# Seven products of a Strassen pair in another order, overlapped with the next pair

## The chip, the cores and the metric

The kernel runs on one core of a Trainium2 chip. The time is device microseconds (us) of one execution of the whole program, lower is better. The engines are named as in the profile: PE is TensorE (PEld its weight loads), DVE is VectorE, ACT is ScalarE, POOL is GpSimd, SP is SyncE, whose queue issues nearly all DMAs. Matmul results land in PSUM, which has eight banks of 128 x 512 floats per core in this kernel's use; all else lives in SBUF or in DRAM.

## The reference, cut to what matters

Two layers of a decoder trunk over 1024 tokens of width 1024, float32. Each layer normalises, projects with one wide matrix, runs four mLSTM heads and four retention heads of width 256, gates them and projects back:

```python
h = rmsnorm(x, norm_g[l]) * (1.0 + scale[:, None, :]) + shift[:, None, :]
p = h @ w_in[l]
mq, mk, mv, mo, mz, mi, mf, rq, rk, rv, rz = split_cols(p)
...
y_m = jax.nn.sigmoid(mo) * head_layernorm(cell, gn_m[l], N_HEADS_MLSTM) * jax.nn.silu(mz)
...
y_r = head_layernorm(ret, gn_r[l], N_HEADS_RET) * jax.nn.silu(rz)
y = jnp.concatenate([y_m, y_r], axis=-1) @ w_out[l]
x = x + gate[:, None, :] * y
```

`cell` and `ret` are chunkwise recurrences over q, k and v. mLSTM's q and k pass a causal convolution of four taps and SiLU first; retention's q and k are rotated by tables of sine and cosine.

## The kernel before, in words

**Precision.** Every float32 product is made of three matmuls on rounded operands (`mm3`): high x high, high x low, low x high. A weight tile is loaded into an `R` tile, `high` (ACT, L381) rounds it into a `wH` tile, `low` (DVE or POOL, L386) puts the rest into another `R` tile. There are 12 `R`, 5 `wH` and 12 `acc` tiles (`acc` is the pool for all 128 x 512 working tiles).

**A pair.** The projection `h @ w_in` is done by pairs of 128-wide column blocks against two halves of 512 tokens, with the contraction of 1024 cut in two. That is a 2 x 2 by 2 x 2 block product, and it is made with seven block products instead of eight (Strassen, in Winograd's form). A product is 4 k-tiles x 3 matmuls of 128 x 512. The weight sides are a11, a12, a22 and sums S1 to S4; the token sides are blocks of h and sums U1 to U4, made once per layer by `build_forms`. Two of the weight sums (S1, S3) are formed by DMAs that accumulate, issued on POOL (L661); S2 and S4 are formed in place by DVE (`total`, L665).

The seven products run into accumulating PSUM banks. `ORDER` says which: X takes a11, then S2, then S3, then a22; Y takes a12; Z takes S1, then S4. After some of them the bank's content so far is copied into an `acc` tile `keep` (ACT, L721) or added with a kept one (DVE, L724 for a12, L728 for S3, L731 for S4), and the sums go on to what uses them: `conv_chain` (ACT L832, DVE L838, L840), `rot_done` (L911 to L913), `z_gate` and `o_gate` (ACT L789 and L798, DVE L791 and L800). The next product into the same bank must wait until the copy or the sum has read it. In a pair X is written by products 1, 3, 5, 7 and Z by 4 and 6, so one product of another bank lies between two of the same. The sum of S3 goes to a fourth bank, those of a12 and S4 stay in theirs. All come from one pool of four banks (`pp`). For values (`vpair_units`) two pairs of heads go side by side, each product in two parts of 24 matmuls of 128 x 256, with three banks per part; `store` (L742 to L751) splits them and writes them to DRAM.

**The order of work.** `plan` lists the pairs (`v` values, `z` and `a` gates, `q` and `k`). `Feeder` turns it into events by product number: loads 7 or 8 products ahead, sums, rounding 3 ahead, low parts 2 ahead. After each product `tick` lets every pending generator do a step: `attention` (one row of `TABLE` per tick, four chunks a head), the chains, `gate_chain` (sums of the mLSTM gates, L503 to L561), `rotary_tables` (L427 to L452), `adaptive`. PE runs exactly in the order written; the instructions of the other engines are put in order by a scheduler that works on priorities (program order, with `tc.high_priority()` ahead) and its own estimate of time. Each engine then runs its queue in order.

**Retention's output.** `values` leaves a chunk's 128 x 256 result in a bank of the other pool (`pa`, four banks); `normalise` takes mean and variance from there (DVE L1119), gets the root from POOL, and ACT scales from the bank (L1139).

**The output projection.** `out_units` takes 16 pieces per half of the tokens and half of the columns (`cc`). `OutLoads.stage` makes a piece when it is taken: it loads the weight tile, rounds it, and with `cc == 0` loads y and its gate (L1208, L1209), multiplies them (DVE L1211), rounds (ACT L1214) and takes the rest (DVE L1215).

Of the kernel before, what the change touches and what calls it, by code (L numbers as in the profile page):

```python
# [11 lines left out]
F32 = mybir.dt.float32  # L12
# [3 lines left out]
ALU = mybir.AluOpType  # L16
# [71 lines left out]
def tile_hybrid_trunk(ctx, tc, x, xt, c, positions, w_ada, b_ada, norm_g, w_in, w_blk, w_val, conv_w, conv_b,  # L88
# [28 lines left out]

    def ps_p():
        return pp.tile([P, 512], F32, tag="p", name=nm("pp"))
# [356 lines left out]
    def gate_chain(l, pgs, gt):  # L476
# [20 lines left out]
        yield 1  # L497
# [125 lines left out]
    NAMES = ("a11", "a12", "S2", "S1", "S3", "S4", "a22")  # L623
    VNAMES = ("a12", "a11", "S2", "S1", "S3", "S4", "a22")
    POOL_LOW = ("S1", "S3", "a22")
    ORDER = (("X", "11"), ("Y", "21"), ("X", "U2"), ("Z", "U1"), ("X", "U3"), ("Z", "22"), ("X", "U4"))
    VORDER = (("Y", "21"), ("X", "11"), ("X", "U2"), ("Z", "U1"), ("X", "U3"), ("Z", "22"), ("X", "U4"))

    class Feeder:
        def __init__(self, now, jobs):  # L630
            self.events, self.forms, self.now = [], [], now
            t = 0
            for add in jobs:
                t = add(self, t)
            self.events.sort(key=lambda e: e[0])
            self.run()
# [9 lines left out]
        def take(self):  # L646
            return self.forms.pop(0)()

        def quad(self, names, blk, t0, u):
            raw, r, h = {}, {}, {}  # L650
            at = {n: t0 + u * i for i, n in enumerate(names)}
# [21 lines left out]
            T2, T4 = at["S2"], at["S3"]  # L673
            ev(T2 - 8, load, "S1", a21)
            ev(T2 - 6, add, "S1", a22)
            ev(T4 - 8, load, "S3", a21)
            ev(T4 - 6, add, "S3", a11)
            for n, src in (("a11", a11), ("a12", a12), ("a22", a22)):
                ev(at[n] - 7 + u, load, n, src)
            for n in names:  # L680
                if n not in ("S2", "S4"):
                    ev(at[n] - 4 + u, hi, n)
                    ev(at[n] - 2, lo, n, G if n in POOL_LOW else V)
            ev(T2 - 4, total, "S2", "a11", "S1")
            ev(T2 - 3, total, "S4", "a12", "S2")
            for n in ("S2", "S4"):
                ev(at[n] - 4 + u, hi, n)
                ev(at[n] - 2, lo, n, V)
            return r, h

    def pair_forms(l, cols2):
        def add(feed, t0):
            blk = [[w_block(l, c, kh) for kh in range(2)] for c in cols2]
            r, h = feed.quad(NAMES, blk, t0, 1)
            feed.forms += [lambda n=n: tiles4(h[n], r[n]) for n in NAMES]
            return t0 + len(NAMES)
        return add

    def vpair_forms(l, heads):
        def add(feed, t0):  # L700
            got = [feed.quad(VNAMES, [[w_val[l, h, kh * 2 + kp] for kh in range(2)] for h in heads], t0, 2)
# [943 lines left out]
```

## Time and profile before

| | |
|---|---|
| time, median of 3 runs (lowest to highest) | 2394.66 us (2390.65 to 2397.98) |
| the profiled execution | 2393.12 us, of which 2391.4 us are the span of the profile |
| PE busy | 2162.7 us, 90% |
| DVE busy | 1820.0 us, 76% |
| ACT busy | 1124.9 us, 47% |
| POOL busy | 948.8 us, 40% |
| granted TensorE clock, mean | 0.962 |
| DMA | 448.32 MB, mean 187 GB/s |

A row of a profile names the line, the engine, the operation and its tiles as out<-in, then busy time and the mean of one instruction; behind the bar stand the idle time of the engine before these instructions and what ended it. In a timeline the idle time before a group stands in square brackets. Lines that begin with SPq are DMA issues.

The span falls into a start (0 to 112 us), layer 0's pairs (to 1011), its output projection (to 1240), layer 1's first projections and gates (to 1300), its pairs (to 2174) and its output projection (to the end).

### The profile page before, as it was taken

To read this page: it belongs to the slowest core of one execution; us is meant where nothing else is said; L and a number is where in the kernel's file an instruction comes from. 1 tells how busy PE (TensorE), PEld (TensorE's weight loads), DVE (VectorE), ACT (ScalarE), POOL (GpSimd) and SP (SyncE) were. 2 spreads that over 40 slices of the span, in tenths; PEclk is the share of its full clock that TensorE was granted. 3 is DMA by queue.
4 is the path that set the end of the run, shared out by engine and by line. 5 is a ranking of instruction groups with operands and counts; after the bars stand their busy time and mean duration, and the time that the engine had idled before them with its cause. 6 is when DMAs were issued, how large, how long until landed. Compare 5 with 4: busy or idle time off the path is not lost. (4 is left out here: it accounts for less than half of the span.)

```text
span 2391.4 us, 35265 instructions
## 1 busy us (share of the span) xinstructions
PE 2162.7 (90%) x11483; PEld 1845.9 (77%) x11483; DVE 1820.0 (76%) x3301; ACT 1124.9 (47%) x2093; POOL 948.8 (40%) x842
## 2 busy tenths in 40 slices
PE   5869999898998999898898799999999999999978
PEld 4668889787897777776686788978977877787756
DVE  5898788979879888763538789788797788977263
ACT  6634334344554565542355334443555555654243
POOL 0333244444443444414165434544544344450303
PEclk8989999999999999999899899999999999999989
DMA  7247678777686667565532686876866666768582
GB/s 249 70 118 227 200 209 250 197 212 203 179 241 160 176 186 202 160 225 195 180 123 75 192 231 167 235 199 173 229 182 173 187 194 180 198 182 245 156 239 100
DMA packets 452549, 448.32 MB, mean 187 GB/s; under 512 B 191218, under 2 KB 309754, under 8 KB 452364
## 3 DMA queue, kind: packets, MB, share of 16 engines
q1 hardware_dynamic: 432636, 410.14, 55.7%
q0 software_dynamic: 19584, 35.66, 9.8%
q8 instruction: 90, 1.47, 0.3%
q14 instruction: 95, 0.78, 0.1%
q10 hardware_dynamic: 144, 0.26, 0.0%
HBM read 322.69 MB, written 123.24 MB: 186 GB/s over the span
## 5 line engine op out<-in xcount | busy, mean ns | idle before, releaser
L155 PE MATMUL pp<-b,wH 128*128 128x512 f32 x1616 | 649.5, 402 | 69.2 <-ACT acc L721 23.4
L156 PE MATMUL pp<-b,wH 128*128 128x512 f32 x1616 | 642.9, 398 | 13.0 <-DVE b L1215 13.0
L157 PE MATMUL pp<-b,R 128*128 128x512 f32 x1616 | 641.5, 397 | 0.0
L381 ACT CAST wH<-R 128x512 fp32r<-128x512 f32 x616 | 376.3, 617 | 451.5 <-PE pp L156 220.4
L386 POOL TENSOR_TENSOR R<-R,wH 128x512 fp32r<-128x512 f32 x276 | 386.8, 1407 | 459.5 <-ACT wH L381 350.3
L155 PEld LDWEIGHTS pp<-b,wH 128*128 128x128 f32 x1616 | 310.7, 192 | 149.5 <-ACT acc L721 38.1
L386 DVE TENSOR_TENSOR R<-R,wH 128x512 fp32r<-128x512 f32 x340 | 278.1, 820 | 159.0 <-ACT wH L381 124.8
L155 PE MATMUL pp<-wH,b 128*128 128x256 f32 (+1 forms) x1024 | 316.5, 309 | 57.3 <-ACT acc L771 19.2
L156 PEld LDWEIGHTS pp<-b,wH 128*128 128x128 f32 x1616 | 310.9, 192 | 73.6 <-DVE b L1215 15.0
L157 PEld LDWEIGHTS pp<-b,R 128*128 128x128 f32 x1616 | 310.2, 192 | 67.7
L156 PE MATMUL pp<-R,b 128*128 128x256 f32 (+1 forms) x1024 | 315.6, 308 | 22.4 <-DVE R L386 22.2
L157 PE MATMUL pp<-wH,b 128*128 128x256 f32 (+1 forms) x1024 | 314.1, 307 | 0.6 <-DVE b L1215 0.6
L155 PEld LDWEIGHTS pp<-wH,b 128*128 128x128 f32 x1024 | 205.3, 200 | 68.4 <-ACT acc L771 20.7
L156 PEld LDWEIGHTS pp<-R,b 128*128 128x128 f32 x1024 | 205.9, 201 | 31.6 <-DVE R L386 26.3
L157 PEld LDWEIGHTS pp<-wH,b 128*128 128x128 f32 x1024 | 205.6, 201 | 7.0 <-DVE b L1215 1.9
L826 POOL TENSOR_TENSOR kc<-acc,kc 128x512 fp32r<-128x512 f32 x64 | 91.0, 1422 | 200.4 <-ACT kc L825 183.5
L661 POOL DMA_DIRECT2D R<-in_w_blk_dram x104 | 92.3, 887 | 139.4 <-DMA R<-in_w_blk_dram 88.8
L838 DVE SCALAR_TENSOR_TENSOR acc<-pp,cols,acc 128x510 f32<-128x510 f32 (+2 forms) x192 | 139.0, 737 | 5.6 <-ACT acc L832 5.5
L826 POOL TENSOR_TENSOR q<-acc,q 128x512 fp32r<-128x512 f32 x64 | 92.6, 1447 | 81.7 <-ACT q L825 80.2
L1031 POOL TENSOR_TENSOR sL<-acc,sH 128x384 fp32r<-128x384 f32 (+1 forms) x64 | 70.8, 1106 | 107.2 <-ACT sH L1030 53.6
L665 DVE TENSOR_TENSOR R<-R,R 128x512 f32<-128x512 f32 x136 | 103.1, 758 | 3.7 <-DMA R<-in_w_blk_dram 1.9
L1054 ACT CAST cH<-cf 128x512 fp32r<-128x512 f32 (+1 forms) x80 | 49.7, 621 | 91.4 <-DVE cf L1051 67.9
(334 smaller groups left out, 4123.0 us busy)
## 6 DMA issues: line engine op xcount, KB each, us to landing
R<-in_w_blk_dram SPq DMA_DIRECT2D x276, 256.0 KB
vdr<-acc SPq DMA_DIRECT2D x128, 256.0 KB
ring<-vdr SPq DMA_DIRECT2D x64, 512.0 KB
R<-in_w_out_dram SPq DMA_DIRECT2D x128, 256.0 KB
R<-in_w_blk_dram POOLq DMA_DIRECT2D x104, 256.0 KB, 4.6
R<-in_w_val_dram SPq DMA_DIRECT2D x80, 256.0 KB
gdr<-acc SPq DMA_DIRECT2D x64, 256.0 KB
acc<-in_w_ada_dram SPq DMA_DIRECT2D x64, 256.0 KB
```

Source lines behind the costliest of these rows:

```text
L155: PE.matmul(o, lt[0], rt[0], start=start, stop=False, skip_group_check=more)
L156: PE.matmul(o, lt[0], rt[1], start=False, stop=False, skip_group_check=more)
L157: PE.matmul(o, lt[1], rt[0], start=False, stop=stop, skip_group_check=more)
L381: A.copy(h, r)
L386: eng.tensor_tensor(lo, r, f(h), ALU.subtract)
L661: G.dma_start(raw[n], src, accum_op=ALU.add)
L665: V.tensor_tensor(raw[n], raw[one], raw[two], ALU.add)
L826: eng.tensor_tensor(dst[1], src, f(dst[0]), ALU.subtract)
L838: V.scalar_tensor_tensor(acc[:, d:], pt[:, 0:HALF - d], wcol, acc[:, d:], ALU.mult, ALU.add)
L1031: G.tensor_tensor(lo, src, f(hi), ALU.subtract)
L1054: A.copy(new[0][:, :, 0:W], cf[:, :, 0:W])
```

## The change

- **Order of the products.** `slot_order` replaces `ORDER`: a11 (X), S1 (Z), the a22 of the pair before (its X), S2 (X), a12 (Y), S4 (Z), S3 (X), and then the next pair. So a pair's a22 comes two products into the next pair. Where values or nothing follow, the pair ends with S3, S4, a22 and has no overlap at its end. Two products of others now lie between two of the same X bank (one at the end of a pair that no pair follows), three between those of Z.
- **Banks.** The pool of four becomes two X banks and two for Y and Z. The sums of S3 and S4 go into the `keep` tiles in SBUF, not to a bank; the chains read them there.
- **Events.** `Feeder` and `quad` take the product numbers from `slot_order`; S4's weight sum is now made after a12 is loaded, from S2's tile.
- **Values.** a22 comes before S4; the a12 product's bank is given back after its sum.
- **Attention** of a head starts 4 instead of 6 ticks after its k pair's last product, which is a22.
- **Retention** copies the result out of the `pa` bank (ACT) into the `n` tile, and `normalise` works on that.
- **Gate sums and rotary tables** start later in the program's order: `gate_chain` pauses 7 ticks instead of 1, `rotary_tables` starts 7 ticks later.
- **Output pieces.** `OutLoads.stage` is split into `fetch` (the loads) and `make` (the arithmetic). Taking a piece keeps two made and three more fetched; the first two are fetched five products before the pairs end and one is made three before.

```diff
+    def ps_x():
+        return pp.tile([P, 512], F32, tag="x", bufs=2, name=nm("px"))
+
+    def ps_z():
+        return pp.tile([P, 512], F32, tag="z", bufs=2, name=nm("pz"))
...
-        yield 1
+        yield 7
...
-    ORDER = (("X", "11"), ("Y", "21"), ("X", "U2"), ("Z", "U1"), ("X", "U3"), ("Z", "22"), ("X", "U4"))
+    PRODUCT = {"a11": ("X", "11"), "S1": ("Z", "U1"), "S2": ("X", "U2"), "a12": ("Y", "21"), "S4": ("Z", "22"),
+               "S3": ("X", "U3"), "a22": ("X", "U4")}
+    VNAMES = ("a12", "a11", "S2", "S1", "S3", "a22", "S4")
+
+    def slot_order(kinds):
+        slots, held = [], []
+        for j, kind in enumerate(kinds):
+            if kind == "v":
+                slots += [(j, n, part) for n in VNAMES for part in range(2)]
+                continue
+            follow = j + 1 < len(kinds) and kinds[j + 1] != "v"
+            slots += [(j, "a11", 0), (j, "S1", 0)] + held + [(j, "S2", 0), (j, "a12", 0)]
+            slots += [(j, n, 0) for n in (("S4", "S3") if follow else ("S3", "S4", "a22"))]
+            held = [(j, "a22", 0)] if follow else []
+        return slots
...
             with tc.high_priority():
-                if n in (0, 2, 3):
+                if n in ("a11", "S1", "S2"):
                     keep[n] = wt("acc", 512, NACC)
-                    A.copy(keep[n], bank["Z" if n == 3 else "X"])
-                elif n == 1:
-                    c = keep[0] if loose else bank["Y"]
-                    V.tensor_tensor(c, bank["Y"], keep[0], ALU.add)
+                    A.copy(keep[n], bank[b])
+                elif n == "a12":
+                    c = keep["a11"] if loose else bank["Y"]
+                    V.tensor_tensor(c, bank["Y"], keep["a11"], ALU.add)
                     done(0, 0, c)
-                elif n == 4:
-                    c = ps_p()
-                    V.tensor_tensor(c, bank["X"], keep[3], ALU.add)
-                    done(1, 1, c)
-                elif n == 5:
-                    V.tensor_tensor(bank["Z"], bank["Z"], keep[2], ALU.add)
-                    done(0, 1, bank["Z"])
+                elif n == "S3":
+                    V.tensor_tensor(keep["S1"], bank["X"], keep["S1"], ALU.add)
+                    done(1, 1, keep["S1"])
+                elif n == "S4":
+                    V.tensor_tensor(keep["S2"], bank["Z"], keep["S2"], ALU.add)
+                    done(0, 1, keep["S2"])
...
-                    src[tt] = po[:, 0:HD]
+                    src[tt] = nrm[j][:, tt, :]
+                    A.copy(src[tt], po[:, 0:HD])
...
         def take(self):
-            self.stage()
+            self.make(2 - len(self.ready))
+            self.fetch(3 - len(self.fetched))
             return self.ready.pop(0)
...
-            launch(rotary_tables())
+            launch(rotary_tables(), 7)
...
+            if sum(left.values()) == 5:
+                loads.fetch(2)
+            elif sum(left.values()) == 3:
+                loads.make()
+            left[j] -= 1
+            if left[j] == 0 and jobs[j][0] == "k":
+                launch(attention(l, jobs[j][1][0], gt), 4, 1)
```

The built programs have the same number of instructions on every engine but ACT, which gets the 64 copies of the retention results. Of the DVE instructions, 204 of 128 columns by about 512 now read two SBUF tiles where they read a PSUM bank and an SBUF tile: 96 taps of the convolution, 28 gate products, 80 products and sums of the rotation and the value split. How the queues move is shown at three places. The line numbers of the changed kernel are higher (L381 becomes L390, L386 L395, L721 L743, L1139 L1158, L1208 L1226).

The first is ACT's queue around one retention q pair of layer 0. The copies (L721, L743) read X and Z; `wH` rows are roundings of weights, `n` rows the retention result, the others attention. Before:

```order
L721 COPY acc_5179<-pp_5166 128x512
L1054 CAST cH_5145<-cf_4719 128x2x256
L381 CAST wH_5300<-R_5160 128x512
L381 CAST wH_5339<-R_5221 128x512
L1139 ACTIVATE n_5134<-pa_5135,nmu_5242,rsd_5199 128x256
L721 COPY acc_5267<-pp_5166 128x512
L1030 CAST sH_5296<-acc_5203 128x384
L1054 CAST cH_5284<-cf_4719 128x2x256
L381 CAST wH_5362<-R_5253 128x512
L721 COPY acc_5320<-pp_5307 128x512
```

And in the changed kernel:

```order
L743 COPY acc_5121<-px_5108 128x512
L1122 COPY n_5139<-pa_5140 128x256
L1072 CAST cH_5151<-cf_4719 128x2x256
L390 CAST wH_5243<-R_5039 128x512
L743 COPY acc_5183<-pz_5170 128x512
L390 CAST wH_5304<-R_5168 128x512
L1158 ACTIVATE n_5139<-n_5139,nmu_5229,rsd_5194 128x256
L390 CAST wH_5345<-R_5106 128x512
L743 COPY acc_5259<-px_5108 128x512
L1048 CAST sH_5298<-acc_5198 128x384
L1122 COPY n_5139<-pa_5275 128x256
```

The copies come in the order a11, S1, S2 now, so that the two from X have Z's between them, and the retention result is taken from its bank by a copy of its own; the scaling that needs `nmu` from DVE still stands in the same queue, ahead of a bank copy.

The second is DVE's queue at layer 0's first value products, with the gate sums (tiles `q`, `kc`, `nd`, `cH`), the token sums (`acc` from `acc`), the weight sums and low parts (`R`) and the first sum of a bank. Before:

```order
L518 COPY cH_1320<-nd_1276 4x512
L520 SCALAR_TENSOR_TENSOR q_1223<-ones,nd_1276 4x512
L512 TENSOR_SCALAR q_1224<-kc_1225 4x512
L665 TENSOR_TENSOR R_1332<-R_1332,R_1340 128x512
L386 TENSOR_TENSOR R_1441<-R_1340,wH_1439 128x512
L613 TENSOR_TENSOR acc_1258<-acc_1258,acc_1256 128x512
L430 TENSOR_SCALAR acc_1196<-acc_1196,kc 128x256
L522 COPY cH_1320<-q_1223 4x512
L523 TENSOR_TENSOR nd_1276<-dm_1226,q_1223 4x512
L514 TENSOR_TENSOR kc_1225<-kc_1225,q_1224 4x512
```

And in the changed kernel:

```order
L527 COPY cH_1584<-nd_1483 4x512
L529 SCALAR_TENSOR_TENSOR q_1219<-ones,nd_1483 4x512
L521 TENSOR_SCALAR q_1220<-kc_1221 4x512
L686 TENSOR_TENSOR R_1303<-R_1303,R_1307 128x512
L395 TENSOR_TENSOR R_1397<-R_1307,wH_1395 128x512
L622 TENSOR_TENSOR acc_1254<-acc_1254,acc_1252 128x512
L792 TENSOR_TENSOR pz_1337<-pz_1337,acc_1424 128x512
L531 COPY cH_1584<-q_1219 4x512
L532 TENSOR_TENSOR nd_1483<-dm_1222,q_1219 4x512
L523 TENSOR_TENSOR kc_1221<-kc_1221,q_1220 4x512
```

The gate sums stand where they stood, between the same weight sums and low parts; the first step of the rotary tables (L430) is gone from here, and the sum of the first value bank (L792, before L772) has come up by 14 rows to this place.

The third is SP's queue in layer 0's output projection, where the pieces of the second half of the tokens begin: `R` rows are weight tiles, `ndr` and `gdr` rows y and its gate, `xdr` rows stores of the residual. Before:

```order
L376 DMA R_12366<-in_w_out_dram 128x512
L376 DMA R_12413<-in_w_out_dram 128x512
L376 DMA R_12440<-in_w_out_dram 128x512
L376 DMA R_12467<-in_w_out_dram 128x512
L1208 DMA acc_12419<-ndr_4_1_100 128x512
L1209 DMA acc_12420<-gdr_4_0_1_140 128x512
L1208 DMA acc_12446<-ndr_4_1_100 128x512
L1209 DMA acc_12447<-gdr_4_1_1_142 128x512
```

And in the changed kernel:

```order
L385 DMA R_12172<-in_w_out_dram 128x512
L1303 DMA xdr_89<-acc_12089 128x512
L385 DMA R_12190<-in_w_out_dram 128x512
L1303 DMA xdr_89<-acc_12098 128x512
L1226 DMA acc_12336<-ndr_4_1_100 128x512
L1227 DMA acc_12337<-gdr_4_0_1_140 128x512
L1303 DMA xdr_89<-acc_12107 128x512
L385 DMA R_12208<-in_w_out_dram 128x512
L1226 DMA acc_12358<-ndr_4_1_100 128x512
```

Before, the first y and gate of the half stood behind 15 weight loads of the column half that runs ahead of it; now 15 weight loads follow them before the fifth piece's y.

217 lines of the change are left out of this document (114 added, 103 removed).

## The prediction

> **What bounds the kernel now.** I read the page's busy times first, then the waits of PE, then the stages.
>
> ```profile
> span 2391.4 us, 35265 instructions
> PE 2162.7 (90%) x11483; PEld 1845.9 (77%) x11483; DVE 1820.0 (76%) x3301; ACT 1124.9 (47%) x2093; POOL 948.8 (40%) x842
> ```
>
> PE is busy nine tenths of the span, and the change gives it the same matmuls. What can be won is its idle time, 2391.4 - 2162.7 = 229 us, and matmuls run at a low clock. The stages (columns: length, busy us and instructions of PE, PEld, DVE, ACT, POOL, then the granted clock and the DMA share):
>
> ```profile
> 112.00:182.00 70.00, 44.98 (x313) 44.05 (x314) 68.24 (x113) 21.95 (x42) 27.14 (x19) 0.80 0.41 120
> 182.00:1011.00 829.00, 773.38 (x4262) 667.88 (x4260) 703.87 (x1328) 402.26 (x770) 352.18 (x327) 0.98 0.71 200
> 1011.00:1240.00 229.00, 199.15 (x859) 161.73 (x857) 104.26 (x178) 90.53 (x150) 78.23 (x61) 0.93 0.58 191
> ...
> 1300.00:1365.00 65.00, 43.36 (x295) 41.97 (x296) 58.94 (x79) 25.47 (x46) 31.66 (x20) 0.84 0.50 145
> 1365.00:2174.00 809.00, 769.98 (x4283) 669.12 (x4282) 661.85 (x1244) 401.33 (x772) 355.70 (x331) 0.98 0.70 194
> 2174.00:2391.40 217.40, 188.20 (x783) 149.13 (x782) 102.47 (x162) 77.06 (x137) 50.95 (x41) 0.95 0.66 191
> ```
>
> Three kinds of stage lose time: the pairs of both layers (55.6 and 39.0 us idle, clock 0.98), the first products of each layer (25.0 and 21.6 us idle, clock 0.80 and 0.84, DVE busy 68 of 70 and 59 of 65 us), and the output projections (29.9 and 29.2 us idle, clock 0.93 and 0.95). Who is waited for in the pairs of layer 0 and then of layer 1:
>
> ```profile
> PE pp L155 <- ACT acc L721: 17.6, 13, 3.6
> PE pp L155 <- DVE pp L728: 9.8, 4, 4.1
> PE pa L155 <- ACT n L1139: 7.8, 5, 2.9
> PE pp L155 <- DVE acc L838: 5.2, 3, 3.3
> PE pp L155 <- ACT acc L771: 3.3, 2, 1.8
> PE pp L155 <- DVE acc L840: 2.8, 3, 1.9
> PE pp L155 <- DVE acc L911: 2.6, 3, 1.5
> ...
> PE pp L155 <- DVE acc L840: 12.8, 6, 3.4
> PE pp L155 <- ACT acc L721: 5.8, 6, 1.6
> PE pa L155 <- ACT n L1139: 5.3, 5, 1.6
> PE pp L155 <- DVE pp L728: 2.8, 3, 1.5
> PE pp L155 <- ACT acc L771: 2.0, 2, 1.8
> PE pp L155 <- DVE acc L911: 0.9, 1, 0.9
> ```
>
> No row names a weight tile (`wH` or `R`): the feeder is early enough, and what PE lacks is a bank. One such wait, by the timelines of PE, ACT and DVE:
>
> ```profile
> 592.66 0.50 PE L155 MATMUL pp<-b,wH 128*128 128x512 f32 x1 [2.48 <-ACT acc L721]
> 589.43 0.51 ACT L1030 CAST sH<-acc 128x384 fp32r<-128x384 f32 x1 [6.40 <-DVE acc L1011]
> 592.03 0.58 ACT L721 COPY acc<-pp 128x512 f32<-128x512 f32 x1
> 582.89 3.54 DVE L386 TENSOR_TENSOR R<-R,wH 128x512 fp32r<-128x512 f32 x1
> ```
>
> A DVE instruction takes 3.54 us, attention's cast on ACT waits 6.40 us for DVE's queue, and the bank copy stands behind it. The copy is short; it is late by its queue, and PE notices as soon as the delay passes one product.
>
> **The change part by part.** A product of pairs takes as long as a piece of the output stage, whose casts follow PE:
>
> ```profile
> 1102.94 0.62 ACT L381 CAST wH<-R 128x512 fp32r<-128x512 f32 x1 [2.10 <-PE pa L156]
> 1105.65 0.62 ACT L381 CAST wH<-R 128x512 fp32r<-128x512 f32 x1 [2.10 <-PE pa L156]
> ```
>
> That is 2.71 us for the same 12 matmuls.
>
> *Bank waits in the pairs.* The rows of L721, L728, L838, L840 and L911 make 38.0 us in layer 0 and 22.3 in layer 1, 60.3 together. Each gets a product more, 2.71 us; only the longest (4.1, 3.6, 3.4, 3.3) pass that, so at most some 56 us go. At the other end nothing goes: PE's gain lets ACT and DVE fall behind by as much. DVE is busy 85% and 82% there, so it has room to follow, but not all; I take six tenths, -36.
>
> *Clock.* Behind waits the clock drops, by the stretches ahead of and behind one:
>
> ```profile
> 562.41 0.80 PE L155 MATMUL pp<-b,wH 128*128 128x512 f32 x1 [2.02 <-ACT acc L721]
> 552.00:562.00 10.00, 6.74 (x30) 5.21 (x30) 8.49 (x17) 5.43 (x11) 5.80 (x8) 1.00 0.81 253
> 562.00:572.80 10.80, 10.39 (x46) 8.79 (x47) 10.80 (x17) 5.59 (x12) 3.50 (x3) 0.84 0.84 242
> ```
>
> 0.16 x 10.8 = 1.7 us lost behind a wait of 2.02 us. A clock of 0.98 over 829 + 809 us is 33 us. I take 14 off; the ends are 0 and 33. The Trainium skill (TensorE: Matmul & The Clock Gate, "Why this matters for your kernels") warns only of idle gaps above about 3 us, since one idle window of about 3.4 us brings the slow clock; by that rule just the four longest waits count, this term would be some -4 and the forecast 2310. The trace differs, 2.02 us were enough, and the measurement decides.
>
> *Retention results.* The bank is freed by a copy instead of by the scaling that waits for `nmu`: of 7.8 + 5.3 us I take 8 off (ends 0 and 13). The 64 copies cost ACT about this each:
>
> ```profile
> L1048 ACT COPY cf<-pa 128x256 f32<-128x256 f32 x16 | 5.9, 373 | 0.0
> ```
>
> 24 us on an engine busy 402 of 829 us; uncovered they would delay the casts and bank copies queued behind them, under 0.4 us each. The scaling still waits in ACT's queue ahead of bank copies.
>
> *Values.* Between S3 and a22 into the same X lies now one product instead of three, as before and after between a11 and S2, whose row is L771: 5.3 us in the pairs' stages. So +4 (ends 0 and +7).
>
> *First products of a layer.* The gate sums are told to start later, but DVE's queue keeps them in place (second order piece): most of these waits stay. The value sums come up by 14 rows; of 46.6 us idle I take 8 off, with 0 and 47 as ends. The last rotary table store stands where it stood in SP's queue, so that costs nothing; if it came later, ACT would wait for it with casts and bank copies behind.
>
> *Output pieces.* All rows of PE's waits for pieces:
>
> ```profile
> PE pp L155 <- ACT b L1214: 27.4, 7, 6.8
> PE pp L156 <- DVE b L1215: 13.0, 5, 4.5
> ```
>
> and the longest in layer 0, with SP's queue:
>
> ```profile
> 1126.22 0.80 PE L155 MATMUL pp<-b,wH 128*128 128x512 f32 x1 [6.82 <-ACT b L1214]
> 1100.43 8.49 SPq L376 DMA_DIRECT2D R<-in_w_out_dram  x4
> 1108.97 0.42 SPq L1208 DMA_DIRECT2D acc<-ndr  x1
> ```
>
> Four weight loads held the queue 8.49 us, each until a tile was free, and y stood behind them; in the third order piece y goes ahead of them. Three pieces ahead are 8 us, more than the longest wait: -28 of 40.4 (ends 0 and 40), and of the clock's 0.07 x 229 + 0.05 x 217 = 27 us another 10 (ends 0 and 27). Loads that need `acc` tiles still queue on SP ahead of others, which keeps the rest.
>
> *DVE's sources.* 204 instructions read two SBUF tiles instead of a bank and a tile. Nearest rows, one form with either source:
>
> ```profile
> L791 DVE SCALAR_TENSOR_TENSOR acc<-acc,pp 128x512 f32<-128x512 f32 x56 | 37.7, 675 | 12.4 <-ACT acc L789 10.9 <-POOL sL L1031 0.8
> L845 DVE SCALAR_TENSOR_TENSOR acc<-acc,acc 128x512 f32<-128x512 f32 x64 | 50.6, 791 | 4.4 <-ACT acc L843 4.4
> ```
>
> 204 x 0.116 = 24 us of DVE, of which I put a quarter on the path: +6 (ends 0 and 24).
>
> Sum: -36 - 14 - 8 + 4 - 8 - 28 - 10 + 6 = -94. The profiled execution took 2393.12 us, 1.5 below the median, so about 2299 against it and 2300 against the median. With all best ends it would be near 2180, with all worst 2425.
>
> **The rivals.**
>
> *DVE sets the pace (0.15).* If DVE can't be kept busier than the 85% of layer 0's pairs, and carries 12 us more per layer, the stages need (704 + 12) / 0.85 = 842 and (662 + 12) / 0.85 = 793 us: +13 and -16, so -3 in place of the -48 of the first four terms and the last: 2345. For it speaks the 3.54 us instruction above, against it 68 of 70 us at the layer's start. The Trainium skill (SBUF — State Buffer, "Who interferes with whom") names the mechanism: a DVE instruction with two SBUF inputs and a POOL instruction that reads SBUF exclude each other. By that rule the change is turned the wrong way for DVE; the two rows above agree in direction, by 0.116 us.
>
> *The earlier fetch changes nothing (0.07),* as the gate sums' later start did: without its 38 us, 2339. The order of SP's queue speaks against.
>
> *Slower (0.12): `acc` tiles run out.* Kept tiles live longer: a11's four products instead of one, S1's from its product to a chain that starts after a22, about ten instead of one. With S2's that is some 19 tile-products a pair instead of 7, so 12 / 7 = 1.7 more of 12 tiles are held. Then attention's loads wait in SP's queue, weight loads behind them. A product's delay in each of the 64 chunks is 173 us; it decides from 35 chunks on (94 / 2.71). With 50 it is -94 + 135 = +41: 2436. Against it, in layer 0's pairs SP waits at these loads only so:
>
> ```profile
> SPq L951 <- POOL dm L981: 1.4, 1, 1.4
> SPq L951 <- DMA qdr<-acc: 1.1, 1, 1.1
> ```
>
> *More than forecast (0.07).* Bank waits (56), their clock (33), retention (13) and output with its clock (67) go whole, the other terms as above: -167, 2228.
>
> **How the numbers follow.** Forecast 0.56, by itself 2262 to 2345 (four to eight tenths of the large terms). With DVE's pace, the useless fetch and the larger gain, faster by over 0.3% has 0.85; a difference under 0.3%, some 7 us, about what a measurement tells from none, gets 0.03 from the edge of the tile rival; slower 0.12. The range 2240 to 2390 leaves out the slower case and the larger gain, 0.19.
>
> **What would show it.** Right: the L721, L728 and L840 rows (L743, L749, L858 in the changed kernel) under 20 us together in the pairs, the clock there 0.99, PE's waits for L1214 and L1215 (L1239, L1240) under 15 us, the layer starts nearly as they were. DVE's pace would show as new PE waits for `R` or `wH` in the pairs with DVE at 85%. Wrong, if SP waits at attention's loads, or if the waits of the pairs come back at other lines.

## The result: 33 us faster, a third of the forecast

The changed kernel takes 2362.69 us (median of 4 runs, 2353.71 to 2371.04) against 2395.92 us (4 runs, 2390.65 to 2397.98) on the same chip: ratio 0.9864, 95% interval 0.9819 to 0.9909. That is -33 us where -94 was forecast. The profiled execution took 2353.71 us, the shortest of the four and 9 us below the median, so the stages below show a little more gain than the medians. Its page:

```profile
span 2352.0 us, 35304 instructions
PE 2150.1 (91%) x11483; PEld 1853.0 (79%) x11483; DVE 1835.5 (78%) x3301; ACT 1146.7 (49%) x2157; POOL 950.8 (40%) x842
```

The stages of the changed kernel (columns as before: length, busy us and instructions of PE, PEld, DVE, ACT, POOL, then granted clock, DMA share, GB/s; the bounds lie at the same places of the program):

```profile
114.60:179.80 65.20, 44.23 (x307) 43.45 (x306) 60.22 (x88) 19.86 (x35) 29.74 (x19) 0.84 0.41 121
179.80:1016.30 836.50, 778.12 (x4270) 676.20 (x4269) 717.53 (x1350) 415.82 (x807) 349.97 (x325) 0.97 0.72 201
1016.30:1206.60 190.30, 185.22 (x839) 153.58 (x839) 98.92 (x171) 88.37 (x147) 76.23 (x60) 0.99 0.65 217
1206.60:1270.70 64.10, 63.38 (x306) 49.22 (x305) 45.38 (x57) 37.64 (x56) 35.58 (x25) 1.00 0.27 70
1270.70:1338.10 67.40, 43.87 (x289) 42.23 (x288) 58.07 (x70) 21.83 (x40) 33.34 (x20) 0.80 0.51 147
1338.10:2165.90 827.80, 773.81 (x4283) 676.08 (x4282) 673.89 (x1257) 416.17 (x813) 352.25 (x330) 0.98 0.69 190
2165.90:2352.00 186.10, 177.21 (x791) 146.49 (x789) 101.97 (x161) 75.71 (x138) 50.78 (x41) 0.99 0.75 218
```

The two output stages lost 38.7 and 31.1 us (from 229.0 and, counted from its first product, 217.2), with the clock at 0.99. The pairs, which should have gained, are longer: 836.5 against 829.0 and 827.8 against 809.2 (counted to the same product), +26 us. The layer starts are about as they were. PE's waits in the pairs of layer 0, then of layer 1, then in layer 0's output stage (us, times, longest):

```profile
PE pa L1092 <- ACT sH L1048: 14.9, 4, 5.0
PE px L164 <- ACT acc L791: 6.8, 3, 2.3
PE pa L166 <- POOL sL L1049: 5.7, 4, 2.5
PE pa L166 <- DVE b L898: 5.1, 4, 2.2
...
PE px L164 <- DVE acc L749: 4.7, 2, 3.9
...
PE px L164 <- ACT acc L743: 1.6, 2, 1.1
...
PE pa L166 <- DVE b L898: 8.3, 3, 4.5
PE px L164 <- ACT acc L791: 7.9, 3, 3.8
PE pa L1010 <- POOL q L844: 5.5, 3, 3.9
PE pa L164 <- DVE nmu L1156: 5.3, 2, 3.4
PE pa L166 <- POOL sL L1049: 5.0, 3, 2.6
PE px L164 <- DVE acc L856: 4.6, 1, 4.6
...
PE px L164 <- ACT acc L743: 4.2, 3, 2.1
...
PE px L164 <- DVE acc L929: 1.4, 1, 1.4
PE px L164 <- DVE acc L749: 1.4, 2, 1.1
...
PE pz L165 <- DVE b L1240: 5.1, 2, 3.5
```

The bank waits of the pairs' copies and sums fell as forecast. In their place stand rows of attention (`pa` banks): PE waits for the cast scores `sH` and `sL`, the k tiles (`b` L898), q, `nmu`. One of these waits, by the timelines of DVE, POOL and PE (a part of the rows):

```profile
1936.99 4.62 DVE L856 SCALAR_TENSOR_TENSOR acc<-acc,cols,acc 128x511 f32<-128x511 f32 x1
...
1942.32 0.87 DVE L898 SCALAR_TENSOR_TENSOR b<-acc,wd,b 128x256 fp32r<-128x256 f32 x2
...
1937.04 1.58 POOL L844 TENSOR_TENSOR q<-acc,q 128x512 fp32r<-128x512 f32 x1
1938.30 2.75 POOL L395 TENSOR_TENSOR R<-R,wH 128x512 fp32r<-128x512 f32 x2
...
1942.85 0.58 PE L166 MATMUL pa<-ring,b 128*128 128x258 f32 x1 [4.55 <-DVE b L898]
```

A convolution step that reads a kept tile stands on DVE for 4.62 us, from 1936.99 to 1941.61. Over nearly all of that time POOL works without a gap (1937.04 to 1941.05), and the step ends 0.56 us after POOL. The k tile that attention needs is queued behind it, and PE waits 4.55 us. The same line by its sources (ns: least, median, most):

```profile
L856 DVE SCALAR_TENSOR_TENSOR acc<-acc,cols,acc x96: 702/743/4622, 574.6 to 2051.9; 128x511 f32<-128x511 f32 x32, 128x510 f32<-128x510 f32 x32, 128x509 f32<-128x509 f32 x32
L856 DVE SCALAR_TENSOR_TENSOR acc<-pz,cols,acc x48: 705/737/749, 571.4 to 2032.9; 128x511 f32<-128x511 f32 x16, 128x510 f32<-128x510 f32 x16, 128x509 f32<-128x509 f32 x16
```

With a bank (`pz`) none is over 749 ns; with a tile the median is the same and the longest six times that. By POOL's timeline, the 33 steps with a tile that have POOL at work for over 60% of their time have a mean of 1.56 us, the 47 with POOL idle 0.74; with a bank (`px` or `pz`) the 28 beside POOL have 0.74. The first theory for the experiments is that *kept tiles as sources cost DVE time*; that POOL is behind it was read from the traces after the first group of runs. Its rivals: attention starts too close behind k, the overlap piles up the chains, or DVE's queue is simply full.

### The profile page after: what moved, and what is told of

Read it like the earlier page. It is cut to its first block, busy times and chain, and to the rows that moved or that the text cites. A ratio compares the mean times of both kernels' runs of the same rounds, so it can differ in the third digit from the quotient of the medians.

```text
span 2352.0 us, 35304 instructions
## 1 busy us (share of the span) xinstructions
PE 2150.1 (91%) x11483; PEld 1853.0 (79%) x11483; DVE 1835.5 (78%) x3301; ACT 1146.7 (49%) x2157; POOL 950.8 (40%) x842
## 5 line engine op out<-in xcount | busy, mean ns | idle before, releaser
L395 POOL TENSOR_TENSOR R<-R,wH 128x512 fp32r<-128x512 f32 x276 | 386.3, 1407 | 479.2 <-ACT wH L390 308.4
L390 ACT CAST wH<-R 128x512 fp32r<-128x512 f32 x616 | 376.3, 617 | 360.9 <-PE px L165 98.5
L164 PE MATMUL px<-b,wH 128*128 128x512 f32 x912 | 362.1, 397 | 11.9 <-DVE acc L749 6.0
L165 PE MATMUL px<-b,wH 128*128 128x512 f32 x912 | 359.8, 395 | 0.0
L166 PE MATMUL px<-b,R 128*128 128x512 f32 x912 | 359.1, 394 | 0.0
L395 DVE TENSOR_TENSOR R<-R,wH 128x512 fp32r<-128x512 f32 x340 | 264.7, 781 | 105.5 <-ACT wH L390 102.5
L165 PE MATMUL pz<-b,wH 128*128 128x512 f32 x704 | 279.2, 397 | 5.1 <-DVE b L1240 5.1
L164 PE MATMUL pz<-b,wH 128*128 128x512 f32 x704 | 279.8, 397 | 0.0
L166 PE MATMUL pz<-b,R 128*128 128x512 f32 x704 | 278.2, 395 | 0.0
L164 PEld LDWEIGHTS px<-b,wH 128*128 128x128 f32 x912 | 174.5, 191 | 50.1 <-ACT acc L743 8.6
L164 PE MATMUL px<-wH,b 128*128 128x256 f32 (+1 forms) x576 | 179.5, 312 | 28.6 <-ACT acc L791 15.5
L166 PEld LDWEIGHTS px<-b,R 128*128 128x128 f32 x912 | 173.7, 190 | 37.6
L165 PE MATMUL px<-R,b 128*128 128x256 f32 (+1 forms) x576 | 178.7, 310 | 24.3 <-DVE R L395 24.3
L165 PEld LDWEIGHTS px<-b,wH 128*128 128x128 f32 x912 | 174.2, 191 | 33.4
L166 PE MATMUL px<-wH,b 128*128 128x256 f32 (+1 forms) x576 | 177.7, 308 | 0.0
L165 PEld LDWEIGHTS pz<-b,wH 128*128 128x128 f32 x704 | 134.9, 192 | 31.6 <-DVE b L1240 5.9
L164 PEld LDWEIGHTS pz<-b,wH 128*128 128x128 f32 x704 | 135.2, 192 | 26.4 <-DVE acc L752 0.3
L164 PE MATMUL pz<-wH,b 128*128 128x256 f32 (+1 forms) x448 | 137.1, 306 | 18.5 <-DVE acc L768 13.8
```

The lines of the kernel that those rows point to most:

```text
L164: PE.matmul(o, lt[0], rt[0], start=start, stop=False, skip_group_check=more)
L165: PE.matmul(o, lt[0], rt[1], start=False, stop=False, skip_group_check=more)
L166: PE.matmul(o, lt[1], rt[0], start=False, stop=stop, skip_group_check=more)
L390: A.copy(h, r)
L395: eng.tensor_tensor(lo, r, f(h), ALU.subtract)
```

## The experiments

Times are medians of 4 runs (7 for the changed kernel with the stretched table); ratios, with their 95% intervals, are to the kernel before on the same chip, and are used across groups; two ratios can be told apart when they differ by some 0.005, or 11 us. The edits are shortened, and what stands behind `#` in them is a remark. "Pair waits" are PE's idle times over both pair stages, summed from its timeline, of attention's banks (`pa`) and of all other banks.

**The parts taken apart.** Output part alone (`e1_out_only`), in the kernel before:

```diff
+        loads = OutLoads(l)          # the changed kernel's class, before the pairs
+                    if (h, arg[1]) == (3, 1) and i == 2: loads.fetch(2)
+                    elif (h, arg[1]) == (3, 1) and i == 4: loads.make()
```

> The kernel before with only the output pieces' part of the change (pieces fetched three ahead and made two ahead, two pieces fetched in the last pair). By the stages of the changed kernel, the two output stages (190.3 and 186.1 us there, 229.0 and 217.2 before) give -70 us and the pairs (836.5 + 827.8 there, 829.0 + 809.2 before) take 26 of it back. If these two are separate, this kernel takes about 2396 - 70 = 2326 us, below both kernels, with pairs of about 1638 us. If the new order of the pairs helps the output stages (attention's tail two products earlier), the output stages stay longer here, some 2340 to 2360. If the pairs of the changed kernel are longer only because the output pieces start in them, pairs here are longer too and the time is about 2350.

Attention later (`e2_later`), in the changed kernel:

```diff
-                launch(attention(l, jobs[j][1][0], gt), 4, 1)
+                launch(attention(l, jobs[j][1][0], gt), 6, 1)
```

> The changed kernel with attention started 6 instead of 4 products after k's last one, the distance it had before. If attention's new waits (sH, sL, the k tiles, q: 41.1 and 33.9 us in the two pair stages, 14.0 and 14.5 before) come from starting two products nearer to the chains that write q and k, they fall to about 30 us together and the time to some 2363 - 35 = 2328. If they come from the backlog of DVE's queue (busy 0.9 to 1.0 in the 12 us ahead of most of them), they stay within 10 us and so does the time: 2355 to 2372.

No overlap (`e3_no_overlap`), in the changed kernel:

```diff
-            follow = j + 1 < len(kinds) and kinds[j + 1] != "v"
+            follow = False           # and attention at 6
```

> The changed kernel without the overlap: each pair ends with S3, S4, a22 of its own, so one product instead of two lies between S3 and a22 in bank X, and attention starts 6 products after k's last one. If the overlap is what lengthens the pairs, they go from 1664 back to some 1640 or below and the time to about 2338. If the overlap does what it is meant to do, PE's waits for the sum of S3 (6.0 us in all now) come back, 15 to 25 us in both layers, and the time is 2370 to 2385. If DVE's queue sets the pace whatever PE's order is, pairs stay at 1655 to 1675 and the time within 10 us of 2363.

Kept tiles in the old order (`e4_sbuf`), on the output part alone:

```diff
-                    c = ps_p()
-                    V.tensor_tensor(c, bank["X"], keep[3], ALU.add)
+                    V.tensor_tensor(keep[3], bank["X"], keep[3], ALU.add)
-                    V.tensor_tensor(bank["Z"], bank["Z"], keep[2], ALU.add)
+                    V.tensor_tensor(keep[2], bank["Z"], keep[2], ALU.add)
```

> The kernel before with the output pieces' part and, in the order of before, the sums of S3 and S4 put into kept tiles instead of a bank, so that the rotary, convolution and gate steps read two tiles instead of a bank and a tile. If that source is what costs (204 instructions at 0.116 us are 24 us of DVE, 12 in each layer), the pairs are 20 to 26 us longer than those of the kernel with the output part alone. If it is a small part, 0 to 8 us; the fourth bank is free earlier, which can give 5 us back.

Measured: output part alone 2330.26 us (0.9744, 0.9713 to 0.9775); attention later 2369.91 (0.9896, 0.9866 to 0.9926); no overlap 2362.97 (0.9885, 0.9846 to 0.9923); kept tiles 2357.29 (0.9849, 0.9815 to 0.9882). The output part alone, pairs and output stage of layer 0, then of layer 1:

```profile
182.90:1018.70 835.80, 775.70 (x4264) 669.69 (x4263) 699.87 (x1332) 402.94 (x772) 352.62 (x326) 0.98 0.72 200
1018.70:1208.50 189.80, 184.72 (x837) 153.02 (x836) 97.24 (x166) 87.06 (x145) 75.12 (x58) 0.99 0.65 217
1336.00:2141.40 805.40, 763.68 (x4272) 663.13 (x4271) 662.57 (x1249) 402.58 (x775) 356.88 (x331) 0.99 0.71 197
2141.40:2327.70 186.30, 177.89 (x795) 147.40 (x793) 101.81 (x160) 75.21 (x136) 52.74 (x41) 0.98 0.76 218
```

Its output stages are as short as the changed kernel's, so they owe nothing to the new order, and all the rest of the change costs some 30 us. Neither the distance of attention nor the overlap accounts for that. Kept tiles do: +27 us in the old order. The pairs of both layers with kept tiles, then the convolution steps with the output part alone and with kept tiles:

```profile
181.90:1022.90 841.00, 779.94 (x4265) 674.15 (x4264) 726.32 (x1332) 403.92 (x772) 357.86 (x327) 0.97 0.72 199
1342.80:2162.40 819.60, 770.85 (x4272) 667.36 (x4271) 677.47 (x1248) 402.39 (x774) 364.34 (x331) 0.98 0.69 192
```

```profile
L838 DVE SCALAR_TENSOR_TENSOR acc<-pp,cols,acc x192: 701/734/752, 563.2 to 2028.0; 128x511 f32<-128x511 f32 x64, 128x510 f32<-128x510 f32 x64, 128x509 f32<-128x509 f32 x64
```

```profile
L837 DVE SCALAR_TENSOR_TENSOR acc<-acc,cols,acc x96: 698/736/3571, 579.3 to 2046.1; 128x511 f32<-128x511 f32 x32, 128x510 f32<-128x510 f32 x32, 128x509 f32<-128x509 f32 x32
```

DVE works 726.32 + 677.47 = 1403.8 us instead of 699.87 + 662.57 = 1362.4, 41 us more with as many instructions, and the span is 20.9 us longer in the profiles, 27 by the medians. The pairs are 19.4 us longer, of which 8.0 are idle time of PE and 11.4 are busy time at the lower clock.

**Is it DVE, and the small edits?** Less work on DVE in the changed kernel (`f1_after_lite`) and in the output part alone (`f2_e1_lite`):

```diff
-                V.tensor_tensor(raw[n], raw[one], raw[two], ALU.add)
+                V.tensor_tensor(raw[n][:, 0:P], raw[one][:, 0:P], raw[two][:, 0:P], ALU.add)
...              # likewise the convolution's and the rotation's last step, the modulation's sums
```

> The changed kernel with less work on DVE in the pairs: four kinds of instructions with two tiles as sources (sums S2 and S4 of the weights, the last step of the convolution and of the rotation, the sums for layer 1's modulation) do 128 of their 512 columns, the rest of the tile is left as it is, so this part of the computation is left out. By their rows this takes some 170 us off DVE, which is busy 1391 of 1664 us in the changed kernel's pairs. If DVE's queue is what PE waits for, whatever the banks do, the waits for attention's steps (75 us in the pairs) fall by more than half and the kernel by 60 us or more, to 2300 or below, and the new order is worth something once DVE is free: it comes out below the next kernel or level with it. If the order itself puts attention too close behind what it needs, the waits stay above 50 us and the time above 2335.

> The kernel with the output part alone (2330 us) with the same work left out on DVE. If DVE's queue is behind the bank waits, they fall here too, by 30 to 50 us, to about 2285 to 2300, and the distance of 33 us to the changed kernel closes (within 10 us, or turned round). If the distance comes from the order and not from DVE, it stays at 25 us or more. If DVE plays no part, neither of the two falls by over 10 us.

Retention's copy (`e5_ret`) and the low part of a12 on POOL (`f4_pool`), each on the output part alone:

```diff
-                    src[tt] = po[:, 0:HD]
+                    src[tt] = nrm[j][:, tt, :]
+                    A.copy(src[tt], po[:, 0:HD])
```

```diff
-    POOL_LOW = ("S1", "S3", "a22")
+    POOL_LOW = ("S1", "S3", "a22", "a12")
```

> The output part and the copy of retention's results out of their bank, nothing else. The forecast gave the copy -8 us; the waits for n are 7.1 us in layer 0's pairs and about as much in layer 1's. Right: the rows for n vanish and the time is some 2322. If 64 more copies on ACT delay the bank copies behind them, or the waits go to the next step, it is within 5 us of 2330 or above.

> The output part, and the low part of a12 made on POOL instead of DVE. This takes about 68 instructions of 0.8 us off DVE (54 us of 1362 in the pairs) and gives POOL as many of 1.4 us. If DVE's queue decides, 10 to 20 us are gained: 2310 to 2320. If POOL's own queue (it makes q, k, sL and the low parts of three weights) becomes late, or its work beside DVE's slows both, it is 2330 or above, with new waits for R, q or sL.

Measured: 2306.90 us (0.9623, 0.9589 to 0.9657), 2274.58 (0.9491, 0.9455 to 0.9526), 2332.90 (0.9725, 0.9688 to 0.9761), 2327.81 (0.9712, 0.9671 to 0.9753). Less work on DVE is worth 58 and 61 us by the ratios, so DVE's queue is on PE's path in both kernels; its busy time in the pairs fell by 124 and 131 us. But the distance of 32 us stays: the theory that the new order comes into its own once DVE has time has fallen. Retention's copy took `pa` waits from 30.3 to 19.7 us and gave 6.1 to the other banks; neither it nor POOL's larger share can be told from the output part alone.

**Places in the queues.** Attention's score steps under `tc.high_priority()`, in the changed kernel (`g1_prio`) and with the output part alone (`g3_e1_prio`); S4's sum left in its bank (`g2_s4bank`, changed kernel); the later starts alone (`g5_delays`, output part alone):

```diff
+                with tc.high_priority():
+                    V.scalar_tensor_tensor(sd[:, 0:CH], ps[:, 0:CH], sc[0], ...
```

```diff
-                    V.tensor_tensor(keep["S2"], bank["Z"], keep["S2"], ALU.add)
-                    done(0, 1, keep["S2"])
+                    V.tensor_tensor(bank["Z"], bank["Z"], keep["S2"], ALU.add)
+                    done(0, 1, bank["Z"])
```

```diff
-        yield 1
+        yield 7                      # gate_chain; rotary_tables launched 7 later
```

> The changed kernel with attention's score steps (the DVE products with the decay and their sum, ACT's sH, POOL's sL) ahead in priority like the bank copies. PE waits 14.9 + 5.7 us for sH and sL in layer 0's pairs, 75 us for all of attention in both. If these waits come from the place that these steps have in the queues, 20 to 35 us are gained: 2328 to 2343. If DVE's queue only passes the delay on to what now stands behind, waits for sH and sL go, others come in their place and the time stays within 10 us of 2363.

> The changed kernel with the sum of S4 left in its bank Z, so that half of the convolutions, gates and rotations that now read two tiles read a bank and a tile again. In the changed kernel a convolution step with two tiles takes 1.56 us where POOL works beside it, 0.74 where not, and with a bank always 0.74. If this source is behind the 27 us that kept tiles cost in the order of before, some 10 to 14 us come back: 2349 to 2353. But Z is to be free for the next pair's S1 three products later: if the chains that read it are late, PE waits for the bank and the gain is lost, 2363 or above.

> The kernel with the output part alone (2330 us) and the same priority for attention's score steps. Its waits for attention are 16 + 14 us in the pairs, so little is to be had: 2322 to 2330 if the place in the queue is what counts. If high priority for these puts the bank copies and low parts back, 2330 to 2345.

> The output part and the later start of the gate sums (7 products instead of 1) and of the rotary tables, alone. The first products of a layer and the gates ahead of them are 120 + 125 us in the kernel with the output part alone. The forecast gave the start of a layer -8 us together with the new order of the values. If the later start counts, 5 to 10 us less: 2320 to 2325. If DVE's queue keeps its order there, within 4 us of 2330.

Measured: 2359.64 us (0.9856, 0.9821 to 0.9891), 2355.59 (0.9837, 0.9813 to 0.9861), 2328.07 (0.9721, 0.9690 to 0.9752), 2337.20 (0.9750, 0.9718 to 0.9782). Priority changes nothing that can be told: the waits for `sH` stay (16.0 us in layer 0's pairs). S4 in its bank takes 14 us from the waits of `pa` and gives 17 to the others (PE now waits for Z's readers); inconclusive. The later starts alone gain nothing (ratio 0.9750 against 0.9744).

**POOL away, and the order by itself.** `h1_order_only` is the changed kernel without retention's copy and the later starts. The other three leave out POOL's low parts, in the changed kernel (`h2_after_nopool`), the output part alone (`h3_e1_nopool`) and kept tiles in the old order (`h4_e4_nopool`):

```diff
-                    src[tt] = nrm[j][:, tt, :]      # order only
-                    A.copy(src[tt], po[:, 0:HD])
+                    src[tt] = po[:, 0:HD]
-        yield 7
+        yield 1                      # and rotary_tables launched at once
```

```diff
-                r[n] = low(h[n], raw[n], eng)      # no POOL low parts
+                r[n] = h[n] if eng is G else low(h[n], raw[n], eng)
```

> The changed kernel without the copy of retention's results and without the later start of the gate sums and rotary tables: the new order with its overlap and kept tiles, and the output part. Against the output part with kept tiles in the order of before (2357 us) it shows the order by itself. If the copy (+3) and the later start (+7) cost what they cost alone, it takes some 2353; if the new order frees PE as forecast (-50 with its clock), 2310; if the order gains nothing, 2357 to 2363.

> The changed kernel without POOL's low parts of the weights (S1, S3 and a22 use the high part twice; this part of the computation is left out). POOL loses about 200 instructions of 1.4 us in the pairs. If DVE's instructions with two tiles cost because they stand still while POOL works, this kernel gains more than the next one by most of the 27 us that kept tiles cost, and comes to within 10 us of it. If POOL is not the cause, the distance of 33 us stays.

> The kernel with the output part alone (2330 us), with POOL's low parts left out in the same way. DVE's instructions with two tiles are longer beside POOL here too (the low parts, the rotation, the small halo steps), so 20 to 50 us should go: 2280 to 2310. If POOL's work costs DVE nothing on PE's path, 2325 to 2335.

> The output part and kept tiles in the order of before (2357 us), with POOL's low parts left out in the same way. If kept tiles cost by POOL, it comes to within 8 us of the kernel before this one, and the distance between this and the changed kernel without POOL's low parts is what the order gives by itself: 0 if nothing, -50 as forecast. If kept tiles cost without POOL, the 27 us stay.

Measured: order only 2357.24 us (0.9856, 0.9827 to 0.9885); without POOL's low parts 2283.60 (0.9561, 0.9529 to 0.9593), 2267.91 (0.9491, 0.9458 to 0.9524) and 2272.05 (0.9505, 0.9479 to 0.9530). Kept tiles now cost 4 us instead of 27 in the old order, and the distance of the changed kernel from the output part alone falls from 32 to 16 us. The convolution steps with kept tiles, then the pairs without and with kept tiles:

```profile
L837 DVE SCALAR_TENSOR_TENSOR acc<-acc,cols,acc x96: 711/742/2060, 558.2 to 1968.7; 128x511 f32<-128x511 f32 x32, 128x510 f32<-128x510 f32 x32, 128x509 f32<-128x509 f32 x32
```

```profile
178.20:975.60 797.40, 764.62 (x4267) 666.11 (x4267) 642.53 (x1332) 405.64 (x773) 216.57 (x229) 0.99 0.75 210
1290.90:2081.60 790.70, 762.96 (x4272) 667.11 (x4271) 612.47 (x1248) 406.86 (x774) 223.47 (x235) 0.98 0.71 200
```

```profile
178.60:980.20 801.60, 765.87 (x4264) 667.59 (x4263) 649.27 (x1329) 405.87 (x770) 218.31 (x228) 0.98 0.74 209
1296.70:2084.00 787.30, 762.30 (x4273) 667.36 (x4272) 612.84 (x1248) 406.62 (x775) 223.00 (x235) 0.98 0.71 201
```

What kept tiles add to DVE's busy time falls from 41 to 7 us. With the output part alone POOL loses 269 us of work, and DVE loses 107 (1362.4 to 1255.0) with as many instructions: so much of DVE's time was spent standing still beside these POOL instructions. The order by itself takes as long as kept tiles in the old order (0.9856 and 0.9849): whatever it gains or costs is below some 11 us, where 50 were forecast. Without POOL's low parts the changed kernel, with its copy and later starts, is still 12 us behind kept tiles in the old order.

**A stretched table for attention** (`i1_after_table`, `i2_e1_table`):

```diff
-    ... "V001", "S1 t1", "U01",
-             "k2 q2 d2", "s1 v2", "V10 U2 m2 K2 Q2", "S2", "k3 d3", "V11 U3", "t2 q3 K3", "s2 v3", "", "V20 U4 m3 Q3",
-             "S3", "", "V21 U5", "", "", "", "V30", "V31", "")
+    ... "V001 t1", "S1", "U01 q2 k2",
+             "d2 s1", "v2 K2 Q2", "m2", "V10 U2 S2", "k3 d3 t2", "q3", "V11 U3 K3 s2", "v3", "Q3", "m3",
+             "V20 U4 S3", "", "", "V21 U5", "", "", "", "V30", "V31")
```

> The changed kernel with attention's table stretched: q and k of chunks 2 and 3 and the k tiles are fetched or split a product earlier, and the products with the state and with sH stand one product later after their scores. In the changed kernel PE's waits for attention's steps are 75 us in the pairs, for banks and others 37. If freed banks gained nothing only because attention's steps had kept their old distance, these waits fall by a third or more and the time by 20 to 35 us, to 2328 to 2343, near the kernel with the output part alone. If the delays are DVE's and come out wherever PE next reads one of its results, the waits change their rows and the time stays within 10 us of 2363.

> The kernel with the output part alone (2330 us) with the same table. Its waits for attention are 30 us in the pairs, for banks and others 72. If attention's distance counts, up to 10 us are gained: 2320 to 2325. If PE's waits only move on to the banks, it stays within 6 us of 2330.

Measured: 2374.65 us (0.9945, 0.9927 to 0.9963) and 2350.10 (0.9854, 0.9825 to 0.9883). The table is no clean test: the next chunk's scores are cast into `sH` before V11 and V21 have read it, so these multiply with the following chunk's scores (that part of the computation is changed), and a new wait for the loads of v came up, 36.8 and 40.0 us over the whole run. The two runs don't answer their question.

**Where PE waits in the pairs:**

| kernel | `pa` | others | sum |
|---|---|---|---|
| before | 28.5 | 65.9 | 94 |
| output part alone | 30.3 | 70.7 | 101 |
| kept tiles, old order | 52.6 | 56.8 | 109 |
| order only | 85.0 | 25.5 | 111 |
| changed kernel | 75.0 | 37.2 | 112 |
| no overlap | 40.0 | 75.1 | 115 |
| priority, changed kernel | 77.1 | 32.1 | 109 |
| S4 in its bank, changed kernel | 61.0 | 54.4 | 115 |
| attention later, changed kernel | 94.8 | 25.6 | 120 |
| less DVE: output part / changed | 11.5 / 58.7 | 53.4 / 26.3 | 65 / 85 |
| on the output part alone: retention's copy / POOL's larger share / priority / later starts | 19.7 / 25.4 / 27.9 / 29.2 | 76.7 / 67.4 / 64.3 / 73.1 | 96 / 93 / 92 / 102 |
| no POOL low parts: output part / kept tiles / changed | 9.3 / 22.3 / 37.7 | 50.9 / 38.4 / 32.1 | 60 / 61 / 70 |

With kept tiles and all of the work (the stretched table apart) the sum is 109 to 120 us in every order; the orders only divide it between the banks and attention. With the sums left in banks it is 92 to 102 us. What DVE and POOL have to do changes it most.

## Why the prediction was wrong

The direction was right, and two steps failed: the price of kept tiles, and the gain from the new order. By the ratios, the output part alone gives -61 us (0.9744), kept tiles take 25 back (0.9849), and the order (0.9856) and then the copy and the later starts (0.9864) add 2 us each, which is nothing that can be told. That makes the -33 that was measured.

*Output pieces, -28, and their clock, -10.* Right in mechanism, mis-sized: the two stages lost 69.8 us. PE's idle time there went from 59 to 14 us and its busy time from 387 to 362, so 45 and 25 us came where 28 and 10 were taken and 40 and 27 stood as ends. The idle time fell by more than its end because what the prediction lists as "All rows of PE's waits for pieces" was not all: some 10 us more were waits in these stages, most of them for weight tiles (`wH` and `R`).

*DVE's sources, +6.* The step that failed is "204 x 0.116 = 24 us of DVE, of which I put a quarter on the path". In the changed kernel's pairs DVE is busy 26 us longer than before (1391.4 against 1365.7), so 24 was near. But in the old order the same kept tiles cost 41 us of DVE and 27 us of time: not a quarter but about two thirds came through, above the upper end of 24. The mean of the second row hid two states. Its steps in the kernel before (ns: least, median, most):

```profile
L845 DVE SCALAR_TENSOR_TENSOR acc<-acc,acc x64: 653/683/1932, 565.6 to 2064.2; 128x512 f32<-128x512 f32 x64
```

The 34 of these with POOL idle have a mean of 0.68 us, the 21 with POOL at work for over 60% of their time 0.93. The 3.54 us instruction of the prediction, which also reads two tiles, stood beside POOL as well, from 582.89 to 586.43:

```profile
583.04 1.59 POOL L386 TENSOR_TENSOR R<-R,wH 128x512 fp32r<-128x512 f32 x1
584.30 1.57 POOL L826 TENSOR_TENSOR q<-acc,q 128x512 fp32r<-128x512 f32 x1
```

The Trainium skill (SBUF — State Buffer, "Who interferes with whom") says that a DVE instruction with two inputs in SBUF contends with a GpSimd instruction that reads SBUF, and that one with at most one SBUF input, outside the 2-port modes, does not. The prediction named this and took the trace to agree "in direction, by 0.116 us"; the steps of the changed kernel agree with both halves: at most 0.75 us with a bank, up to 4.62 with a tile beside POOL.

*Bank waits in the pairs, -36, and the clock, -14.* The rows did fall: L743, L749, L856 and L929 come to 18.3 us where 60.3 stood, and the three rows that the sign names to 11.8, under its 20. But the step "DVE is busy 85% and 82% there, so it has room to follow" failed: the waits at attention's banks rose by 46.5 us, and the order by itself is worth nothing that can be told. The prediction's "what PE lacks is a bank" said too much already of the kernel before: beside the rows for n, its `pa` banks had 15.4 us of waits for attention's own steps, which the sum does not price. The largest, in layer 0 and then in layer 1:

```profile
PE pa L992 <- POOL q L826: 2.5, 2, 1.6
PE pa L155 <- DVE acc L1020: 2.1, 2, 1.3
...
PE pa L1074 <- POOL sL L1031: 4.4, 3, 3.0
PE pa L992 <- POOL q L826: 2.1, 3, 1.1
```

These grew to 75.0 us. That the bank was only the first place where PE met a late result of DVE fits this, but no run singles it out. The clock term came to nothing, with 0.97 and 0.98 in the pairs where 0.98 stood in both. It was argued from one wait of 2.02 us, with a clock of 0.84 behind it, but the length of a wait does not settle the clock: in the kernel before, one of 3.33 us lies in a stretch at 1.00.

```profile
642.64 0.36 PE L155 MATMUL pp<-wH,b 128*128 128x256 f32 x1 [3.33 <-DVE acc L838]
639.00:650.00 11.00, 7.67 (x64) 7.50 (x63) 10.83 (x27) 5.33 (x11) 3.99 (x5) 1.00 0.37 109
```

The prediction's sign for the wrong case, "if the waits of the pairs come back at other lines", is what happened.

*Retention, -8:* the rows for n went, others took their place. *Values, +4:* the row that gave the price (L791 now) is 14.7 us in the pairs instead of 5.3, over the upper end; but it is the wait between a11 and S2, which are as near as before, and the pair that came nearer, S3 and a22 (L799), costs only 1.0. *First products, -8:* 65.2 and 67.4 us against 70.0 and 65.0, so -2.

*The rivals.* DVE's pace came nearest for the pairs: 842 and 793 us at 85%, 836.5 and 827.8 measured; but that is -3 against the +26 that came, and only layer 0 fits. Its signs, waits for `R` or `wH`, did not show; the waits came at attention, at 86% and 81% of DVE. The `acc` tiles did not run out: at attention's loads of q and k into `acc` tiles the longest waits of SP are for k's own stores, in layer 0 and layer 1, and no other row there is over 2.7 us:

```profile
SPq L882 <- DMA kdr<-acc: 3.4, 2, 2.4
```

```profile
SPq L882 <- DMA kdr<-acc: 5.4, 3, 3.4
```

*What stays open.* That DVE's lateness comes partly from standing still beside POOL is shown. Why an order that frees banks does not lower the sum of waits is not: that attention's steps lack distance fits the table of waits, but starting attention later did not help, and the one test with the table was spoiled. POOL's own lateness is a rival that no run separates: 24.1 us of the 75.0 are waits for POOL's results (`sL`, q and the k parts, 9.1 before), and leaving out its low parts shortens its queue, too, so not all of the 62 us gained there need have come through DVE. The version that beats both kernels is the old order with the output part alone, 2330 us.

## What to carry to other kernels

Before moving a result from a bank into a tile, ask who reads it: in this kernel a DVE step with two tiles could stand still for as long as POOL worked on tiles, and the mean hid that, so look at the longest step, too. Waits that go at one buffer can come back at another, so count the sum of waits over the stage: in these pairs the new order moved it about, and only less work for DVE or POOL made it clearly smaller. Parts of a change that touch different stages are best priced and run apart.

## What the runs showed that was not expected

DVE may stand still over several POOL instructions in a row (4.62 us above), and a small step is no exception: in the changed kernel with less work on DVE a step of 128 x 2 took 2.96 us, beside two of POOL's that took 2.83 together:

```profile
846.58 2.96 DVE L858 SCALAR_TENSOR_TENSOR acc<-halo,cols,acc 128x2 f32<-128x2 f32 x1
```

```profile
846.68 2.83 POOL L395 TENSOR_TENSOR R<-R,wH 128x512 fp32r<-128x512 f32 x2
```
